# Two banks instead of one for keys, queries and rotary queries, and one step more in a statistic

## The chip, the cores and the metric

The kernel runs on one core of a Trainium2 chip. The time is device microseconds of one execution; before the change the median of three runs is 2838.42 us, from 2837.55 to 2839.09. A core has a matrix engine (TensorE, PE in the rows; PEld is its weight load), VectorE (DVE), ScalarE (ACT), GpSimd (POOL) and SyncE (SP), whose queue issues nearly all transfers. Each engine works its instructions in the order written for it and waits where an operand is not there yet.

## The reference, cut to what matters

Two layers over 256 tokens of width 2048 in float32: a mixer, a convolutional feed-forward network and a gated embedding in each. The change touches the latent attention in the mixer of the first layer:

```python
q = (rmsnorm(cq, q_a_norm) @ w_uq).reshape(b, s, 8, 192)      # 128 plain, 64 rotary
kv = (rmsnorm(ckv, kv_a_norm) @ w_ukv).reshape(b, s, 8, 256)
k_nope, v = kv[..., :128], kv[..., 128:]
k = concat([k_nope, broadcast(kpe)]);  q = rmsnorm(q, q_norm);  k = rmsnorm(k, k_norm)
q, k = rope on the last 64 columns;    o_b = causal_attention(q, k, v)
```

`cq` and `ckv` have 512 columns, so each of these projections sums over four chunks of 128.

## The kernel before, in words

Features lie on the 128 partitions, tokens along the free dimension. A product of float32 quality is made of three products of a shorter format: high weights by high input, high weights by low input, low weights by high input. An input tile holds its high part in columns 0 to 255 and its low part in columns 256 to 511. Weights arrive as blocks of 128 x 1024 (`raw`); ScalarE casts the high part `wh` (line 160, three buffers), VectorE subtracts for the low part `wl` (line 166, four buffers).

Two helpers turn a block into 256 output features. `gemm_fm` (line 174) takes two PSUM banks, one per 128 features: eight products of 512 columns with `wh` (line 190; high and low input at once, so a bank ends with two halves), then eight of 256 columns with `wl` (line 192), at the latest after two blocks. Its result is gathered by `evac` (line 299): per bank ScalarE copies one half to `evt` (line 302) and VectorE adds the other half (line 303). `gemm_fm1` (line 203) takes one bank and issues three products of 256 columns per chunk and half (lines 215, 217, 218), all summed in place; the result can be used as it is. The pool `mm` has five banks.

Work that follows a product is a Python generator. `spawn` starts it, and `pump` lets every live generator take one step; `gemm_fm` pumps after the high products of each block, `gemm_fm1` at the end of each block. `steps(n)` in a generator passes n pumps. `token_stats` (line 358) is such a generator: column sums of squares (`sm_col`, line 368), the power on GpSimd (line 330), diagonal matrices `dg` (line 346), two steps, then two products that spread the row over all partitions (`sm_bc`, line 354). A scheduler then fixes the order of each engine from these pieces; it may place an instruction somewhat before or behind where the text issues it.

The latent attention (`mla`, line 771) goes: values of heads 0 to 3; two rotary-query products (`q_rope`, line 810), each followed by a rotation (`sm_rot`, line 779, then GpSimd and VectorE, lines 309 and 782); then four rounds `up(n)`: keys, queries, and two attention heads spawned. Between the rounds `fill` puts one output product of the other mixer (`xa` by `w_eo0`, 16 high and 16 low products over two blocks). `keys` squares its result on ScalarE (line 836), GpSimd adds the squared rotary key (line 840), TensorE sums the columns (`sm_hs`, line 790); `queries` does the same with two half additions on GpSimd (line 860).

Of the kernel before, what the change touches and what calls it, by code (L numbers as in the profile page):

```python
# [78 lines left out]
def hybrid_kernel(ctx, tc, io):  # L79
# [42 lines left out]
    def spawn(g):  # L122
        if next(g, active) is not active:
            active.append(g)

    def finish():
        while active:
            pump()

    def steps(n):  # L130
        for _ in range(n):
            yield
# [172 lines left out]
    def bcast(row, n=2):  # L305
        return row.unsqueeze(1).to_broadcast([P, n, T])

    def mul(dst, a, b, engine=None):
        (engine or nc.vector).tensor_tensor(dst, a, b, op=ALU.mult)
# [11 lines left out]
    def small(shape, name):  # L321
        return psum.tile(shape, F32, tag="sm", name=name, bufs=3)
# [32 lines left out]
                             start=(half == 0), stop=(half == 1))  # L355
        nc.scalar.copy(dst, ps[:, 0:n * P])

    def token_stats(acc, n, wait=0):

        r = {}  # L360

        def chain():
            yield from steps(wait)
            if acc.shape[1] == 2:
                nc.vector.tensor_tensor(acc[:, 0], acc[:, 0], acc[:, 1], op=ALU.add)
            ps = small([P, 512], "sm_col")
            for m in range(2):
                nc.tensor.matmul(ps[:, m:m + 1], acc[:, 0, m * P:(m + 1) * P], mcol("ones")[:, 0:1],
                                 start=True, stop=True)
            c = rstd_from(ps[:, 0:2], [P, 2], n)  # L370
            r["col"] = c
            dg = diagonals(c, (0, 1))
            yield from steps(2)
            bc = npool.tile([P, T], F32, tag="rbc", name="rbc", bufs=3)
            bcast_rows(dg, bc)
            r["bc"] = bc
        spawn(chain())
        return r
# [293 lines left out]
    def even_mixer(rs, xs):  # L672
# [3 lines left out]
        with tc.tile_pool(name="low", bufs=2) as low:  # L676
            shift(low, "low")
            kpe = low.tile([P, 1, T], F32, name="kpe", bufs=1)
            with tc.tile_pool(name="l0a", bufs=2) as pool:
                hvs = {}  # L680
                done = {}

                def proj(ps, tag, key):
                    yield from until(rs, "bc")
                    y = pool.tile([P, 2, T], F32, tag=tag, name=tag, bufs=2)
                    mul(y, ps, bcast(rs["bc"]))
                    done[key] = y

                def proj_halves(ps, tag, key):
                    yield from until(rs, "bc")  # L690
                    y = pool.tile([P, 2, T], F32, tag=tag, name=tag, bufs=2)
                    evac(ps, y)
                    mul(y, y, bcast(rs["bc"]))
                    done[key] = y

                def values(ps, g):
                    yield from until(rs, "col")
                    hv = pool.tile([P, 2, 512], F32, tag="hv", name="hv", bufs=2)
                    for m in range(2):
                        nc.scalar.activation(hv[:, m], ps[m], AF.Copy, scale=rs["col"][:, m:m + 1])  # L700
                    hvs[g] = hv

                def pair(hp):
                    yield from until(done, (hp, 2))
                    yield from hgrn_pair(pool, hp, done[hp, 0], done[hp, 1], done[hp, 2], lbc, hvs, mix_a)

                lbc = None
                for hp in range(HG_HEADS // 2):
                    if hp == 0:
                        for g, ps in enumerate(first):  # L710
                            spawn(values(ps, g))
                        nc.sync.dma_start(out=mat, in_=io["mat"])
                        nc.vector.tensor_copy(ones_r, mcol("ones"))
                        nc.sync.dma_start(out=vec, in_=io["vec"])
                        lbc = lower_bounds(pool)
                    for k, tag in enumerate(("hf", "hq", "hg")):
                        if hp == 0 and k == 0:
                            spawn(proj(gemm_fm1(io["w_hg"][0], xs), tag, (hp, k)))
                        else:
                            spawn(proj_halves(gemm_fm(io["w_hg"][3 * hp + k], xs), tag, (hp, k)))  # L720
                    if hp == 0:
                        spawn(rope_tables(pool))
                    spawn(pair(hp))


                def low_rank(ps, n, gain, acc, chunks):
                    y = low.tile([P, 2, T], F32, tag="ly", name="ly")
                    evac(ps, y)
                    mul(y, y, bcast(rs["bc"]))
                    if n == 0:  # L730
                        nc.scalar.activation(acc, y, AF.Square)
                    else:
                        sq = npool.tile([P, 2, T], F32, tag="sq", name="sq")
                        nc.scalar.activation(sq, y, AF.Square)
                        nc.vector.tensor_tensor(acc, acc, sq, op=ALU.add)
                    for j in range(2):
                        x = low.tile([P, 2 * T], F32R, name=f"x_{gain}{2 * n + j}", bufs=1)
                        split(x, y[:, j], vcol(gain, 2 * n + j))
                        chunks.append(x)

                stat = {}
                chunks = {"kva": [], "qa": []}
                for part, gain in ((1, "kva"), (0, "qa")):
                    acc = low.tile([P, 2, T], F32, tag="lacc", name="lacc", bufs=1)
                    for n in range(2):
                        low_rank(gemm_fm(io["w_low"][2 * part + n], xs), n, gain, acc, chunks[gain])
                    stat[gain] = token_stats(acc, 512, 2)
                    if part == 1:
                        ps = gemm_fm1(io["w_kpe"], xs, ncol=1, kb=8)
                        mul(kpe, ps, bcast(rs["bc"], 1))  # L750
                while len(mix_a) < HG_HEADS:
                    pump()
                heads_a = iter(range(NC // 2))

                def fill(count=1):

                    for _ in range(count):
                        n = next(heads_a)
                        residual(n, gemm_fm(io["w_eo0"][n], [mix_a[c] for c in range(HG_HEADS)]))

                fill(2)
                finish()
# [9 lines left out]
    def mla(pool, kpe, ckv, cq, rkv, rqa, mix, fill):  # L772
# [37 lines left out]
        def q_rope(ps, g):  # L810
            yield from until(rqa, "bc")
            y = pool.tile([P, 2, T], F32, tag="ly", name="ly")
            mul(y, ps, bcast(rqa["bc"]))
            sq = pool.tile([P, 2, T], F32, name=f"sqr{g}", bufs=1)
            nc.scalar.activation(sq, y, AF.Square)
            nc.scalar.activation(y, y, AF.Copy, scale=vcol("qr"))
            yield
            z = pool.tile([P, 2, T], F32, name=f"qr{g}", bufs=1)
            rotate(z, y)
            for j in range(2):  # L820
                sqr[2 * g + j] = sq[:, j]
                qr[2 * g + j] = z[:, j]
# [8 lines left out]
        def keys(ps, n):  # L831
            yield from until(rkv, "bc")
            y = pool.tile([P, 2, T], F32, tag="ly", name="ly")
            mul(y, ps, bcast(rkv["bc"]))
            sq = npool.tile([P, 2, T], F32, tag="sq", name="sq")
            nc.scalar.activation(sq, y, AF.Square)
            z = pool.tile([P, 2, T], F32, tag="kn", name="kn", bufs=3)
            nc.scalar.activation(z, y, AF.Copy, scale=vcol("kn"))
            lo = sq[0:64]
            nc.gpsimd.tensor_tensor(lo, lo, sqk[0:64].unsqueeze(1).to_broadcast([64, 2, T]), op=ALU.add)  # L840
            yield from steps(2)
            r = pair_rstd(sq, 1.0)
            dg = diagonals(r, (0, 2, 1, 3))
            yield from steps(2)
            rk = pool.tile([P, 2, T], F32, tag="rk", name="rk", bufs=2)
            bcast_rows(dg, rk.rearrange("p a t -> p (a t)"))
            pairs["k", n] = (z, rk)

        def queries(ps, n):
            yield from until(rqa, "bc")  # L850
            y = pool.tile([P, 2, T], F32, tag="ly", name="ly")
            mul(y, ps, bcast(rqa["bc"]))
            sq = npool.tile([P, 2, T], F32, tag="sq", name="sq")
            nc.scalar.activation(sq, y, AF.Square)
            z = pool.tile([P, 2, T], F32, tag="qn", name="qn", bufs=3)
# [57 lines left out]
            mix[hh] = x  # L913

        def up(n):
            spawn(keys(gemm_fm1(io["w_uk"][n], ckv), n))
            spawn(queries(gemm_fm1(io["w_uq"][n], cq), n))
            for j in range(2):
                spawn(attention(n, j, 2 * j))

        spawn(values(gemm_tm(io["w_uv"][0], ckv), 0))
        for g in range(2):
            spawn(q_rope(gemm_fm1(io["w_uqr"][g], cq), g))
        up(0)
        fill()
        up(1)
# [286 lines left out]
```

## Time and profile before

| what | value |
|---|---|
| median of three runs | 2838.42 us |
| the profiled execution's own time | 2838.33 us |
| its span, first to last instruction | 2836.5 us |
| TensorE busy | 2828.3 us (100%) |
| VectorE busy | 1904.7 us (67%) |
| ScalarE busy | 1412.2 us (50%) |
| GpSimd busy | 85.8 us (3%) |
| mean granted TensorE clock | 1.000 |

The profile comes from one execution. A busy time counts an engine as occupied from an instruction's start to its end; matmuls overlap each other, so the pace of TensorE is read from start to start and not from the length of one. In a wait, the name behind the arrow is the work that ended last before the waiting one could start.

### The profile page before, as it was taken

The page shows a single profiled execution, that of the slowest core. Times are in us where ns is not written, and L with a number is a line of the kernel's source. Part 1 is how long each engine was busy: PE and PEld are TensorE (multiplying, and loading weights), DVE is VectorE, ACT ScalarE, POOL GpSimd, SP SyncE. Part 2 cuts the span into 40 slices and gives each one's busy share as a digit, 9 for nine tenths or more (in the row PEclk, how much of TensorE's full clock was granted, in tenths as well). Part 3 has the DMA queues.
Part 4 walks back from the last instruction along what each step waited for, and adds up shares of the span by engine and source line. Part 5 has one row for each costly group of instructions (what it writes and reads, how often), then busy time and mean ns, then how long its engine had stood idle before and what let it go on. Part 6 is the DMA issues. An engine that isn't in the chain of part 4 may idle for free.

```text
span 2836.5 us, 41173 instructions
## 1 busy us (share of the span) xinstructions
PE 2828.3 (100%) x15993; PEld 2471.9 (87%) x15993; DVE 1904.7 (67%) x2777; ACT 1412.2 (50%) x1864; POOL 85.8 (3%) x123
## 2 busy tenths in 40 slices
PE   9999999999999999999999999999999999999999
PEld 7888888888888888888888888888888888888888
DVE  7876787766557666776565555556777755777666
ACT  5765555444344444565544444455444433444444
POOL 1110300000000000000000000000000000000000
PEclk9999999999999999999999999999999999999999
DMA  7545445665656665565555555555656665566565
GB/s 240 179 156 164 133 154 187 192 192 189 190 188 192 192 189 190 182 196 182 184 182 187 189 187 186 185 183 183 193 186 193 192 190 190 186 193 193 186 193 164
DMA packets 147941, 525.60 MB, mean 185 GB/s; under 512 B 16544, under 2 KB 18336, under 8 KB 147744
## 3 DMA queue, kind: packets, MB, share of 16 engines
q1 hardware_dynamic: 147600, 522.95, 58.2%
q8 instruction: 125, 2.05, 0.3%
q14 instruction: 72, 0.59, 0.1%
q10 hardware_dynamic: 144, 0.01, 0.0%
HBM read 520.80 MB, written 2.10 MB: 184 GB/s over the span
## 4 chain that ended last, share of the span: by engine, by line
PE 98%; DVE 1%; DMA 0%; issue 0%; ACT 0%; POOL 0%; SPq 0%; DVEq 0%
PE mm L190 52%; PE mm L192 27%; PE mm L235 4%; PE mm L234 4%; PE mm L236 4%; PE sm_ro L1015 1%; PE mm L215 0%; PE mm L218 0%; PE mm L217 0%; PE mm L271 0%; PE mm L272 0%; PE mm L270 0%; DVE wl L166 0%; PE sm_sc L881 0%; PE sm_rt L1029 0%; PE sm_sc L880 0%
## 5 line engine op out<-in xcount | busy, mean ns | idle before, releaser
L160 ACT CAST wh<-raw 128x1024 fp32r<-128x1024 f32 (+1 forms) x990 | 1032.5, 1044 | 1196.2 <-PE mm L190 766.3
L166 DVE TENSOR_TENSOR wl<-raw,wh 128x1024 fp32r<-128x1024 f32 (+1 forms) x848 | 1025.2, 1217 | 646.4 <-ACT wh L160 629.6
L190 PE MATMUL mm<-xs,wh 128*128 128x512 f32 x4288 | 1028.9, 391 | 0.1
L190 PEld LDWEIGHTS mm<-xs,wh 128*128 128x128 f32 x4288 | 787.2, 188 | 153.2 <-DVE xs L318 0.4
L192 PEld LDWEIGHTS mm<-xs,wl 128*128 128x128 f32 x4288 | 541.4, 189 | 19.1
L192 PE MATMUL mm<-xs,wl 128*128 128x256 f32 x4288 | 550.9, 281 | 0.0
L190 PE MATMUL mm<-hs,wh 128*128 128x512 f32 x1408 | 337.2, 391 | 0.0
L190 PEld LDWEIGHTS mm<-hs,wh 128*128 128x128 f32 x1408 | 258.2, 188 | 49.6
L166 DVE TENSOR_TENSOR wlt<-raw,wh 128x1024 fp32r<-128x1024 f32 x142 | 175.4, 1236 | 145.6 <-PE mm L235 124.3
L234 PE MATMUL mm<-wh,xs 128*128 128x512 f32 x512 | 199.7, 390 | 0.0
L235 PE MATMUL mm<-wlt,xs 128*128 128x512 f32 x512 | 199.3, 389 | 0.0
L236 PE MATMUL mm<-wh,xs 128*128 128x512 f32 x512 | 199.2, 389 | 0.0
L192 PEld LDWEIGHTS mm<-hs,wl 128*128 128x128 f32 x1408 | 179.4, 189 | 7.3
L192 PE MATMUL mm<-hs,wl 128*128 128x256 f32 x1408 | 181.7, 281 | 0.0
L302 ACT COPY evt<-mm 128x256 f32<-128x256 f32 x300 | 98.3, 375 | 92.1 <-PE mm L192 92.1
L190 PE MATMUL mm<-xo,wh 128*128 128x512 f32 x512 | 122.7, 391 | 0.0
L236 PEld LDWEIGHTS mm<-wh,xs 128*128 128x128 f32 x512 | 96.1, 188 | 20.0
L234 PEld LDWEIGHTS mm<-wh,xs 128*128 128x128 f32 x512 | 96.1, 188 | 19.5
L235 PEld LDWEIGHTS mm<-wlt,xs 128*128 128x128 f32 x512 | 96.2, 188 | 19.4
L190 PEld LDWEIGHTS mm<-xo,wh 128*128 128x128 f32 x512 | 94.0, 188 | 18.5 <-DVE xo L1032 0.3
L406 DVE TENSOR_TENSOR h<-h,mm 128x256 f32<-128x256 f32 x128 | 48.2, 416 | 37.2 <-PE mm L192 37.2
L192 PEld LDWEIGHTS mm<-xo,wl 128*128 128x128 f32 x512 | 64.9, 189 | 2.5
(283 smaller groups left out, 2040.4 us busy)
## 6 DMA issues: line engine op xcount, KB each, us to landing
raw<-in_wg SPq DMA_DIRECT2D x176, 512.0 KB, 3.7
raw<-in_wu SPq DMA_DIRECT2D x176, 512.0 KB, 4.0
raw<-in_wd SPq DMA_DIRECT2D x176, 512.0 KB, 3.8
raw<-in_w_oqk SPq DMA_DIRECT2D x64, 512.0 KB, 4.0
raw<-in_w_ov SPq DMA_DIRECT2D x64, 512.0 KB, 3.6
raw<-in_w_og SPq DMA_DIRECT2D x64, 512.0 KB, 3.6
raw<-in_w_oo SPq DMA_DIRECT2D x64, 512.0 KB, 3.9
raw<-in_wpg SPq DMA_DIRECT2D x60, 512.0 KB, 3.8
```

The costliest lines, as they stand in the source:

```text
L160: nc.scalar.copy(wh, raw)
L166: nc.vector.tensor_tensor(wl, raw, wh.bitcast(F32), op=ALU.subtract)
L190: nc.tensor.matmul(ps[j], w[:, o:o + P], xs[kc], start=(kc == 0), stop=False)
L192: nc.tensor.matmul(ps[j][:, 0:T], w[:, o:o + P], xs[kc][:, 0:T], start=False, stop=(kc == n - 1))
L234: nc.tensor.matmul(ps[m], xh, wh[:, o:o + 512], start=(kc == 0), stop=False)
L235: nc.tensor.matmul(ps[m], xh, wl[:, o:o + 512], start=False, stop=False)
L236: nc.tensor.matmul(ps[m], xl, wh[:, o:o + 512], start=False, stop=(kc == n - 1))
L302: nc.scalar.copy(tmp[:, j], ps[j][:, T:2 * T])
L406: nc.vector.tensor_tensor(h[i][:, j], h[i][:, j], ps[j][:, 0:T], op=ALU.add)
L1015: nc.tensor.matmul(pso, at[:, c, o:o + P], v[:, b, s], start=(n == 0), stop=(n == len(terms) - 1))
```

## The change

Three edits. `token_stats` takes the number of its inner steps as an argument, and the statistic of the keys and values (`kva`, part 1) passes three instead of two. The products of keys, queries and rotary queries (four, four and two of them, one block each) go from `gemm_fm1` to `gemm_fm`: two banks, eight products of 512 columns and eight of 256 where there were 24 of 256. Their three consumers get the two halves, so each gathers them with `evac` first and multiplies the gathered tile in SBUF, where it multiplied the bank directly.

```diff
-    def token_stats(acc, n, wait=0):
+    def token_stats(acc, n, wait=0, more=2):
...
-            yield from steps(2)
+            yield from steps(more)
...
-                    stat[gain] = token_stats(acc, 512, 2)
+                    stat[gain] = token_stats(acc, 512, 2, 3 if part == 1 else 2)
...
         def q_rope(ps, g):
             yield from until(rqa, "bc")
             y = pool.tile([P, 2, T], F32, tag="ly", name="ly")
-            mul(y, ps, bcast(rqa["bc"]))
+            evac(ps, y)
+            mul(y, y, bcast(rqa["bc"]))
...
         def keys(ps, n):
-            mul(y, ps, bcast(rkv["bc"]))
+            evac(ps, y)
+            mul(y, y, bcast(rkv["bc"]))
...
         def queries(ps, n):
-            mul(y, ps, bcast(rqa["bc"]))
+            evac(ps, y)
+            mul(y, y, bcast(rqa["bc"]))
...
         def up(n):
-            spawn(keys(gemm_fm1(io["w_uk"][n], ckv), n))
-            spawn(queries(gemm_fm1(io["w_uq"][n], cq), n))
+            spawn(keys(gemm_fm(io["w_uk"][n], ckv), n))
+            spawn(queries(gemm_fm(io["w_uq"][n], cq), n))
...
-            spawn(q_rope(gemm_fm1(io["w_uqr"][g], cq), g))
+            spawn(q_rope(gemm_fm(io["w_uqr"][g], cq), g))
```

Outside the stretch from this statistic to the end of the attention heads, each engine's order is as before. Three places of it follow; line numbers behind line 810 are one to three higher in the changed kernel.

TensorE at the statistic of keys and values, before: `sm_bc` spreads the row, `xs` by `wh` and `wl` are high and low products of the next low-rank projection.

```order
L368 MATMUL sm_col<-mat,lacc 128x1 x2
L190 MATMUL mm<-xs,wh 128x512 x16
L192 MATMUL mm<-xs,wl 128x256
L354 MATMUL sm_bc<-dg,ones_r 128x256
L192 MATMUL mm<-xs,wl 128x256 x2
L354 MATMUL sm_bc<-dg,ones_r 128x256
L192 MATMUL mm<-xs,wl 128x256 x13
```

The same place in the changed kernel:

```order
L368 MATMUL sm_col<-mat,lacc 128x1 x2
L190 MATMUL mm<-xs,wh 128x512 x16
L192 MATMUL mm<-xs,wl 128x256 x16
L190 MATMUL mm<-xs,wh 128x512 x8
L354 MATMUL sm_bc<-dg,ones_r 128x256 x2
```

The two spreading products stand 15 low and eight high products later.

TensorE from the end of the first queries into the first `fill`, before: `xa` is the fill, the first `sm_hs` the column sums of the first keys, the second those of the first queries.

```order
L218 MATMUL mm<-x_qa_2740,wl 128x256
L190 MATMUL mm<-xa,wh 128x512 x8
L790 MATMUL sm_hs<-mat,sq 128x1 x4
L190 MATMUL mm<-xa,wh 128x512 x8
L790 MATMUL sm_hs<-mat,sq 128x1 x4
L192 MATMUL mm<-xa,wl 128x256 x16
```

In the changed kernel, from the second rotation on (`sm_rot`, which stood ahead of the queries' products before):

```order
L779 MATMUL sm_rot<-ly,mat 128x512
L190 MATMUL mm<-x_qa_2634,wh 128x512
L190 MATMUL mm<-x_qa_2737,wh 128x512 x2
L190 MATMUL mm<-x_qa_2740,wh 128x512 x2
L192 MATMUL mm<-x_qa_2631,wl 128x256 x2
L192 MATMUL mm<-x_qa_2634,wl 128x256 x2
L192 MATMUL mm<-x_qa_2737,wl 128x256 x2
L192 MATMUL mm<-x_qa_2740,wl 128x256 x2
L190 MATMUL mm<-xa,wh 128x512 x9
L790 MATMUL sm_hs<-mat,sq 128x1 x4
L190 MATMUL mm<-xa,wh 128x512 x7
L192 MATMUL mm<-xa,wl 128x256 x6
```

The second rotation has moved behind the third product of the queries (the first one, likewise, behind the ninth product of the keys), while the keys' sums stand nine products into the fill, where it was eight.

VectorE in the same stretch, before: `ly<-mm,rbc` is the multiplication of a finished projection, `qr` the rotation, `wl` a weight block.

```order
L309 TENSOR_TENSOR ly<-mm,rbc 128x512
L309 TENSOR_TENSOR qr_2987<-sm_rot,sin_mla 128x512
L166 TENSOR_TENSOR wl<-raw,wh 128x1024
L782 TENSOR_TENSOR qr_2987<-qr_2987,ly 128x512
L309 TENSOR_TENSOR ly<-mm,rbc 128x512
L309 TENSOR_TENSOR qr_3029<-sm_rot,sin_mla 128x512
L166 TENSOR_TENSOR wl<-raw,wh 128x1024
L782 TENSOR_TENSOR qr_3029<-qr_3029,ly 128x512
```

In the changed kernel, where `ly<-mm,evt` is the addition of `evac` and `ly<-ly,rbc` the multiplication:

```order
L309 TENSOR_TENSOR qr_2970<-sm_rot,sin_mla 128x512
L166 TENSOR_TENSOR wl<-raw,wh 128x1024
L782 TENSOR_TENSOR qr_2970<-qr_2970,ly 128x512
L309 TENSOR_TENSOR qr_3010<-sm_rot,sin_mla 128x512
L303 TENSOR_TENSOR ly<-mm,evt 128x256
L782 TENSOR_TENSOR qr_3010<-qr_3010,ly 128x512
L303 TENSOR_TENSOR ly<-mm,evt 128x256
L309 TENSOR_TENSOR ly<-ly,rbc 128x512
```

The first keys' multiplication, the last row here, stood ahead of the second rotation's two VectorE instructions and now stands behind them.

## Rows read from the trace of the kernel before

**Rows 1.** The page: busy time by engine; the chain that ended last, by engine.
```profile
PE 2828.3 (100%) x15993; PEld 2471.9 (87%) x15993; DVE 1904.7 (67%) x2777; ACT 1412.2 (50%) x1864; POOL 85.8 (3%) x123
...
PE 98%; DVE 1%; DMA 0%; issue 0%; ACT 0%; POOL 0%; SPq 0%; DVEq 0%
```

**Rows 2.** Waits of TensorE, whole span: total us, times, longest.
```profile
PE spin L99 <- DVE cold L96: 1.1, 1, 1.1
...
PE sm_bc L354 <- DVE dg L346: 0.6, 1, 0.6
```

**Rows 3.** Timeline of TensorE at the statistic: start, length, instruction, idle before.
```profile
243.32 0.28 PE L192 MATMUL mm<-xs,wl 128*128 128x256 f32 x1
244.23 0.35 PE L354 MATMUL sm_bc<-dg,ones_r 128*128 128x256 f32 x1 [0.63 <-DVE dg L346]
```

**Rows 4.** Timeline of VectorE at the same place.
```profile
244.00 0.48 DVE L346 TENSOR_SCALAR dg<-mat,rl 128x128 fp32r<-128x128 f32 x2
```

**Rows 5.** Timeline of TensorE in an undisturbed stretch of the two-bank product.
```profile
389.82 3.82 PE L190 MATMUL mm<-xb,wh 128*128 128x512 f32 x16
393.48 2.05 PE L192 MATMUL mm<-xb,wl 128*128 128x256 f32 x16
395.36 3.82 PE L190 MATMUL mm<-xb,wh 128*128 128x512 f32 x16
```

**Rows 6.** Timeline of TensorE: rotary queries, first rotation, first keys, the keys' sums.
```profile
281.13 0.28 PE L218 MATMUL mm<-x_qa,wl 128*128 128x256 f32 x1
...
286.55 1.02 PE L779 MATMUL sm_rot<-ly,mat 128*128 128x512 f32 x2
...
287.52 0.28 PE L217 MATMUL mm<-x_kva,wh 128*128 128x256 f32 x1
...
295.76 0.95 PE L790 MATMUL sm_hs<-mat,sq 128*128 128x1 f32 x8
```

**Rows 7.** Windows: stretch, its length, busy us of PE, PEld, DVE, ACT, POOL, clock, DMA.
```profile
280.00:290.00 10.00, 10.00 (x78) 9.38 (x76) 7.19 (x10) 6.88 (x9) 2.04 (x2) 1.00 0.50 159
```

**Rows 8.** Timeline of VectorE, from the last low-rank projection to the first fill.
```profile
263.46 0.75 DVE L303 TENSOR_TENSOR ly<-mm,evt 128x256 f32<-128x256 f32 x2
264.24 0.69 DVE L309 TENSOR_TENSOR ly<-ly,rbc 128x512 f32<-128x512 f32 x1
...
287.61 0.69 DVE L309 TENSOR_TENSOR qr<-sm_rot,sin_mla 128x512 f32<-128x512 f32 x1 [0.17 <-PE sm_rot L779]
288.21 1.82 DVE L166 TENSOR_TENSOR wl<-raw,wh 128x1024 fp32r<-128x1024 f32 x1
289.96 0.68 DVE L782 TENSOR_TENSOR qr<-qr,ly 128x512 f32<-128x512 f32 x1
...
293.64 1.77 DVE L782 TENSOR_TENSOR qr<-qr,ly 128x512 f32<-128x512 f32 x1
```

**Rows 9.** Timeline of ScalarE, same stretch.
```profile
251.93 0.65 ACT L302 COPY evt<-mm 128x256 f32<-128x256 f32 x2 [0.72 <-PE mm L192]
...
283.80 1.05 ACT L160 CAST wh<-raw 128x1024 fp32r<-128x1024 f32 x1 [1.51 <-PE mm L217]
...
285.42 0.73 ACT L816 ACTIVATE ly<-ly,vec 128x512 f32<-128x512 f32 x1
...
291.47 0.63 ACT L836 ACTIVATE sq<-ly 128x512 f32<-128x512 f32 x1
```

**Rows 10.** Timeline of GpSimd, from the second rotation into the second round.
```profile
291.34 1.30 POOL L309 TENSOR_TENSOR ly<-ly,cos_mla 128x512 f32<-128x512 f32 x1 [2.38 <-PE sm_rot L779]
292.60 2.26 POOL L840 TENSOR_TENSOR sq<-sq,sqk 64x512 f32<-64x512 f32 x1
296.75 1.79 POOL L860 TENSOR_TENSOR sq<-sq,sqr 64x256 f32<-64x256 f32 x2 [1.90 <-ACT sq L854]
298.62 1.01 POOL L330 TENSOR_TENSOR rr<-rv,mat 128x4 f32<-128x4 f32 x1
...
307.77 1.48 POOL L840 TENSOR_TENSOR sq<-sq,sqk 64x512 f32<-64x512 f32 x1 [4.10 <-ACT sq L836]
```

## The prediction

> **What bounds the kernel now.** I read the page first. TensorE is busy all the time, and the chain that ended last is its own to 98% [rows 1]. So nothing counts but what TensorE issues, at what pace, and where it stands still; VectorE, ScalarE and GpSimd cost only where they make it wait. The waits of TensorE came next: over the whole span the largest is 1.1 us in total, at the very start, and one of 0.6 us stands before the spreading product of a statistic [rows 2]. There is therefore little to win by removing waits, and any new wait is paid in full. Then the timeline: TensorE at the statistic [rows 3] and in the two kinds of product [rows 5, 6], and the other three engines where the changed projections are consumed [rows 7 to 10]. There the reader is to see that VectorE (7.19 of 10 us) and ScalarE (6.88) have some three microseconds of room in ten [rows 7].
>
> All sums are made against the profiled execution, 2838.33 us; the median of the three runs is 0.09 us more, which I neglect.
>
> **The step more in the statistic.** From the low product at 243.32 to the spreading product at 244.23 pass 0.91 us [rows 3]. The pace of such products is 0.12 us: sixteen take 395.36 - 393.48 = 1.88 us [rows 5]. So 0.79 us are lost, to the diagonals, which end at 244.48 [rows 4]. In the changed order the pair stands 15 low and eight high products later, 15 x 0.1175 + 8 x 0.229 = 3.6 us after 243.4, at about 247.0, when the diagonals have long been there. The row that it makes is first used on the keys' product, which begins at about 287 [rows 6], 40 us later, so nothing is late next. Gain 0.79 us, whole.
>
> **Ten products in two banks.** One block was 24 products of 256 columns. From 281.13 to 286.55 there are 46 starts in 5.42 us, 0.1178 us each [rows 6], 2.83 us a block. Now there are eight of 512 columns, (393.48 - 389.82) / 16 = 0.229 us each, and eight of 256 at 0.1175 [rows 5]: 2.77 us. That is 0.057 us a block, 0.57 us for ten. The columns are as many as before; only starts are saved.
> The Trainium skill, page "TensorE: Matmul & The Clock Gate", section "Back-to-back issue gap", gives an isolated warm gap of N/2.4 + 2.5 ns, 109 and 216 ns here; by an estimate from it a block would save 0.02 us and the ten 0.2 us. The starts measured here are dearer (118 and 229 ns), so I keep 0.57.
>
> **What the gathering adds.** Per projection, two copies on ScalarE (0.65 us [rows 9]) and two additions on VectorE (0.75 [rows 8]); the multiplication stays at 0.69. In the densest stretch, two rotary products, first keys and first queries in some 11 us, this is 3.0 us for VectorE, whose room is about as large. Weights are prepared more than a block ahead (the cast at 283.80 [rows 9] is of the queries' block, which follows the keys of 287.52 [rows 6]), and low products now come behind eight high ones, 1.83 us, so I cost weights at nothing; what hides them is that lead. What I do not cost at nothing are the chains from one projection's result to the next TensorE instruction that needs it, since the order has the latter at nearly the same place:
>
> First rotation. It needs ScalarE's scaled tile. ScalarE, in its order: a weight cast that can begin when the second rotary product's last high product is done (0.39 after its start: 3.82 - 15 x 0.229 [rows 5]), cast 1.05, copy 0.33, square 0.63, copy 0.33, scale 0.73 [rows 9]: 3.46 us. TensorE in that time: 0.23 + 0.94 (eight low) + 1.83 (eight high of the keys) + 0.12 (one low) = 3.12. It waits 0.34 us (0.1 to 0.6).
>
> Keys' sums, round one. The keys' multiplication now stands on VectorE behind the second rotation's addition, and that waits for GpSimd. From the start of the second rotation: result to dependent 287.61 - 286.55 = 1.06 [rows 6, 8], GpSimd 1.30 [rows 10], addition 0.68, gathering addition 0.38, multiplication 0.69 [rows 8], square 0.63 [rows 9], GpSimd's addition 1.48 to 2.26 [rows 10]: 6.2 to 7.0 us. TensorE: the rotation 0.85 (287.52 - 286.55 less one start [rows 6]), five high 1.15, eight low 0.94, nine high of the fill 2.06: 5.0 us. It waits 1.2 to 2.0 us, up to 2.5 if the weight block ahead of it on VectorE is slowed as at 288.21 (1.82) [rows 8]. I take 1.7, since a weight block starts on VectorE just before GpSimd's addition, as where that took 2.26. Behind the waiting sums stand the rest of the fill and everything after: nothing overtakes.
>
> Queries' sums, round one. GpSimd now computes the keys' power before the queries' additions, and the power waits for the keys' sums. From their end: 1.01 + 1.79 [rows 10] and about 0.5 of hand-overs (estimate: half of the 1.06 us above), 3.3 us; TensorE has seven high, six and two low products and a sum, 1.60 + 0.94 + 0.2 = 2.7. It waits 0.5 (0 to 0.8).
>
> Round two. The queries' gathering stands on VectorE behind an instruction that waits for the keys' sums: 0.5 + 0.75 + 0.69 + 0.63 + 1.79 = 4.4 us to the queries' sums, against five high products, three transposes (0.4, estimate by the 0.95 of the sums' eight [rows 6]) and fifteen low, 3.3. It waits 1.0 (0 to 2.0). Rounds three and four have a whole product or more between these points, by the order 5 to 8 us against chains of 4 to 6 (estimates with the same durations): nothing (0 to 1.5 each).
>
> Banks: five, two a projection now. The fill's second bank is the keys' first, freed 2.1 to 2.9 us after the second rotation; TensorE is there after 2.94. Nothing, but without spare.
>
> Sum: -0.79 - 0.57 + 0.34 + 1.7 + 0.5 + 1.0 = +2.2 us, 2838.33 + 2.2 = 2840.5 us. With the lower ends of the waits (0.1 + 1.2) it is 2838.3, with the upper ones (0.6 + 2.5 + 0.8 + 2.0 + 3.0 = 8.9) 2845.9.
>
> **The rivals.**
> Covers hold: the sums find their operands ready and only the gains stay, 2838.33 - 1.36 = 2837.0 us. For it: before the change GpSimd's addition ended at 294.86 and the sums started at 295.76 [rows 6, 10], 0.9 us of room. Against it: the chain is longer by two rows on VectorE and a wait for GpSimd. Chance 0.15.
>
> Rounds three and four wait as well, 1.0 us each: 2842.5 us. For it: VectorE is given 0.75 us more in each projection; against it: the transposes, scores and outputs that stand between. Chance 0.12.
>
> Slower: VectorE and GpSimd stop each other. A rotation addition took 0.68 us at 289.96 and 1.77 at 293.64, where GpSimd's addition ran beside it, and a weight block took 1.82 beside GpSimd's 1.30 [rows 8, 10]. The ten multiplications took a bank and an SBUF tile and now take two SBUF tiles. If each meets GpSimd and stands on the path, 10 x 1.09 = 10.9 us more, 2851 us; it decides from four of the ten on (2.2 + 4.4 us is beyond 0.2%). Against it: GpSimd works 85.8 us in all [rows 1], and the next chain often waits for the multiplication, so that GpSimd is idle then. Chance 0.07.
> The Trainium skill, "SBUF — State Buffer", section "Who interferes with whom", says that a VectorE instruction with two SBUF inputs contends with a GpSimd instruction that reads SBUF, and one with a bank as input does not; the 1.77 and 1.82 us agree with it, and by it the change trades ten free instructions for ten exposed ones.
>
> The forecast itself, some waits on the sums of rounds one and two: chance 0.66, its own range 2838.3 to 2842.5.
>
> **How the numbers follow.** The three runs spread 1.5 us; 0.2%, 5.7 us, is about what a measurement can tell from no change. Forecast and the first two rivals lie within it. Slower by more is the third, 0.07; faster by more has no mechanism here, with 1.4 us of gains and no wait above 1.1 us left to remove [rows 2], and gets 0.02 for what I overlook; 0.91 is left. The range goes from the first rival, 2836.9, to 2843.4, short of the upper ends' sum.
>
> **What the profile of the changed kernel would show.** The spreading pair without idle time before it; blocks of keys and queries 2.77 us long; a gap of some 0.3 us before the first rotation; keys' sums of round one starting 1 to 2 us after the ninth product of the fill, released by GpSimd; less before the queries' sums of rounds one and two. If those sums start at once, the first rival is right; if gaps follow in rounds three and four, or multiplications of 1.5 us and more appear, the others. A gap before a `wh` or `wl` product would show that the weights' lead did not last.

## The result, and the profile of the changed kernel

The changed kernel takes 2843.32 us in the median of 16 runs (2842.20 to 2845.42); the kernel before, run beside it on the same chip, 2838.19 us (16 runs, 2837.34 to 2839.65). The ratio is 1.0019, with a 95% interval of 1.0012 to 1.0026. The change makes the kernel 5.1 us slower; 2.2 us were forecast. The profiled execution took 2844.31 us with a span of 2842.5 us, 6.0 us more than the span before. The difference of the medians is a little smaller, and the changed kernel's runs scatter more; a reason for the scatter comes with the experiments. Three single runs in the experiments below, of 4160 us and more, are left out of every ratio.

The page first: busy time by engine, and the chain that ended last, by engine.

```profile
PE 2831.7 (100%) x15913; PEld 2471.3 (87%) x15913; DVE 1913.6 (67%) x2797; ACT 1417.9 (50%) x1884; POOL 86.4 (3%) x123
...
PE 97%; DVE 1%; issue 1%; POOL 1%; DMA 0%; ACT 0%; SPq 0%; POOLq 0%; DVEq 0%
```

Against [rows 1] TensorE has 80 products fewer and yet is busy 3.4 us longer, and GpSimd has come into the chain. Fewer products that take longer is the first sign of something that the forecast had no term for. The waits of TensorE over the whole span (total us, times, longest):

```profile
PE sm_hs L790 <- POOL sq L842: 2.5, 1, 2.5
PE sm_hs L790 <- POOL sq L863: 1.1, 3, 0.5
```

The wait of 0.6 us before the spreading product [rows 2] is gone, and 3.6 us of waits on GpSimd before the head sums (`sm_hs`) are new. The timeline of TensorE shows them in place; the columns are start, length, instruction, and idle time before it:

```profile
247.21 0.40 PE L354 MATMUL sm_bc<-dg,ones_r 128*128 128x256 f32 x2
...
287.63 0.28 PE L192 MATMUL mm<-x_kva,wl 128*128 128x256 f32 x1
287.84 1.13 PE L779 MATMUL sm_rot<-ly,mat 128*128 128x512 f32 x2
...
290.32 1.03 PE L779 MATMUL sm_rot<-ly,mat 128*128 128x512 f32 x2
...
293.26 2.23 PE L190 MATMUL mm<-xa,wh 128*128 128x512 f32 x9
297.94 1.62 PE L790 MATMUL sm_hs<-mat,sq 128*128 128x1 f32 x8 [2.45 <-POOL sq L842]
299.42 3.33 PE L190 MATMUL mm<-xa,wh 128*128 128x512 f32 x7
302.56 1.48 PE L192 MATMUL mm<-xa,wl 128*128 128x256 f32 x6
303.83 0.42 PE L790 MATMUL sm_hs<-mat,sq 128*128 128x1 f32 x2
...
305.46 1.17 PE L192 MATMUL mm<-xa,wl 128*128 128x256 f32 x8
306.47 0.86 PE L190 MATMUL mm<-x_kva,wh 128*128 128x512 f32 x3
...
311.77 2.00 PE L190 MATMUL mm<-x_qa,wh 128*128 128x512 f32 x8
...
314.56 2.00 PE L190 MATMUL mm<-xa,wh 128*128 128x512 f32 x8
...
324.19 0.38 PE L790 MATMUL sm_hs<-mat,sq 128*128 128x1 f32 x2 [0.47 <-POOL sq L863]
...
325.06 0.83 PE L790 MATMUL sm_hs<-mat,sq 128*128 128x1 f32 x6 [0.27 <-POOL sq L863]
325.75 0.48 PE L234 MATMUL mm<-wh,x_kva 128*128 128x512 f32 x1
...
368.28 0.83 PE L790 MATMUL sm_hs<-mat,sq 128*128 128x1 f32 x6 [0.38 <-POOL sq L863]
```

The reader is to see two things. The keys' sums of round one begin at 297.94, where nine products from 293.26 at 0.229 us each [rows 5] would have brought them to 295.32: 2.6 us of standing still. (The profile's 2.45 counts from the modelled end of the last product.) And behind that wait the same instructions are slow: seven products of 512 columns occupy 299.42 to 302.56, 0.449 us each, where the eight at 311.77 are done in the usual 2.00 us. The windows show why (stretch, length, busy us of PE, PEld, DVE, ACT, POOL, granted clock, DMA):

```profile
290.00:300.00 10.00, 7.55 (x37) 5.86 (x36) 8.55 (x13) 5.72 (x11) 4.43 (x4) 0.91 0.35 119
300.00:310.00 10.00, 10.00 (x47) 8.55 (x45) 7.07 (x19) 2.49 (x3) 4.25 (x4) 0.75 0.19 54
```

The same stretches in the kernel before:

```profile
290.00:300.00 10.00, 10.00 (x68) 8.87 (x67) 7.41 (x12) 6.58 (x8) 6.25 (x5) 1.00 0.50 158
300.00:310.00 10.00, 10.00 (x74) 8.92 (x73) 7.76 (x22) 2.78 (x4) 4.08 (x3) 1.00 0.41 126
```

The granted clock, 1.00 in both stretches before, is 0.91 and then 0.75 of full speed here. A full clock is 2.4 GHz and the lower level 1.2, so 0.09 and 0.25 missing of ten microseconds are 1.8 and 5.0 us at the lower level: 6.8 us, from about 298.2, right behind the wait, to about 305.0. The low products at 305.46 are at their usual pace again (eight in 1.17 us, with one change of product before them). The page's row of 40 slices doesn't show it, since each slice is 71 us long.

What made the sums late stands on the other engines. VectorE, then GpSimd, then ScalarE, same columns:

```profile
289.61 1.82 DVE L166 TENSOR_TENSOR wl<-raw,wh 128x1024 fp32r<-128x1024 f32 x1
...
293.22 0.69 DVE L782 TENSOR_TENSOR qr<-qr,ly 128x512 f32<-128x512 f32 x1 [0.26 <-POOL ly L309]
293.83 0.42 DVE L303 TENSOR_TENSOR ly<-mm,evt 128x256 f32<-128x256 f32 x1
294.28 0.69 DVE L309 TENSOR_TENSOR ly<-ly,rbc 128x512 f32<-128x512 f32 x1
...
296.69 1.75 DVE L309 TENSOR_TENSOR ly<-ly,rbc 128x512 f32<-128x512 f32 x1
```

```profile
291.44 1.75 POOL L309 TENSOR_TENSOR ly<-ly,cos_mla 128x512 f32<-128x512 f32 x1 [1.09 <-PE sm_rot L779]
295.71 2.17 POOL L842 TENSOR_TENSOR sq<-sq,sqk 64x512 f32<-64x512 f32 x1 [2.53 <-ACT sq L838]
```

```profile
295.00 0.63 ACT L838 ACTIVATE sq<-ly 128x512 f32<-128x512 f32 x1 [0.86 <-DVE ly L309]
```

From the second rotation (290.32) to the sums (297.94) the chain takes 7.62 us. It is link by link the one that the forecast laid out, with the rotation's GpSimd part at 1.75 us where [rows 10] had 1.30.

A ledger by four places in TensorE's order, each start compared with its start before: the first fill product of round one comes 0.66 us earlier than before (293.26 against 293.92), the first keys' product of round two 5.21 us later (306.47 against 301.26), and the first products behind round two's sums 6.51 us later (325.75 against 319.24); at the end it is 6.0. The three starts before:

```profile
293.92 2.00 PE L190 MATMUL mm<-xa,wh 128*128 128x512 f32 x8
...
301.26 0.28 PE L215 MATMUL mm<-x_kva,wh 128*128 128x256 f32 x1
...
319.24 0.40 PE L234 MATMUL mm<-wh,x_kva 128*128 128x512 f32 x1
```

So the loss is made in two places: 5.87 us in round one's sums, 1.30 us in round two's; everything behind gives back 0.5 us net.

### The profile page after: what moved, and what is told of

The parts are those of the page before. It is cut to its first block, busy times and chain, and to the rows that moved or that the text cites. A ratio compares the mean times of both kernels' runs of the same rounds, so it can differ in the third digit from the quotient of the medians.

```text
span 2842.5 us, 41055 instructions
## 1 busy us (share of the span) xinstructions
PE 2831.7 (100%) x15913; PEld 2471.3 (87%) x15913; DVE 1913.6 (67%) x2797; ACT 1417.9 (50%) x1884; POOL 86.4 (3%) x123
## 4 chain that ended last, share of the span: by engine, by line
PE 97%; DVE 1%; issue 1%; POOL 1%; DMA 0%; ACT 0%; SPq 0%; POOLq 0%; DVEq 0%
PE mm L190 53%; PE mm L192 27%; PE mm L234 4%; PE mm L235 4%; PE mm L236 4%; PE sm_ro L1018 1%; PE mm L271 0%; PE mm L272 0%; PE mm L270 0%; PE sm_rt L1032 0%; PE sm_ra L994 0%; PE sm_sc L884 0%; DVE wl L166 0%; DMA raw<-in_w_hv 0%; PE sm_o L648 0%
## 5 line engine op out<-in xcount | busy, mean ns | idle before, releaser
L302 ACT COPY evt<-mm 128x256 f32<-128x256 f32 x320 | 104.7, 374 | 96.6 <-PE mm L192 96.6
```

The source lines that it names most:

```text
L302: nc.scalar.copy(tmp[:, j], ps[j][:, T:2 * T])
```

## The experiments

All kernels are timed in five rounds beside the kernel before, whose median was 2838.34 us with the first four (the step alone, the idle products, the longer GpSimd work, the sums one step later), 2838.04 with the next four (the banks alone, the longer work with idle products, the addition on VectorE, four steps and three) and 2838.21 with the other two (rotary queries in one bank, four steps and two). Theory: a wait of 2.6 us and a clock that falls behind it. Rivals: the two-bank products are slow in themselves, or the work of the other engines is.

**The step alone.** The kernel before with only the step more in the statistic.

```
-    def token_stats(acc, n, wait=0):
+    def token_stats(acc, n, wait=0, more=2):
...
-            yield from steps(2)
+            yield from steps(more)
...
-                    stat[gain] = token_stats(acc, 512, 2)
+                    stat[gain] = token_stats(acc, 512, 2, 3 if part == 1 else 2)
```

> The kernel before with the step more in the key-value statistic and nothing else. Both theories (the loss is the wait for the first keys' sums plus the slow clock behind it; or the loss belongs to the two-bank products and their gathering as such) give the gain of the prediction's first term, 0.8 us: 2837.4 us against 2838.2, no idle time before the spreading pair, clock 1.00 throughout. If the step only moved the wait elsewhere: 2838.2.

Measured: 2837.23 us (11 runs, 2836.63 to 2838.99), ratio 0.9997 [0.9988, 1.0005], span 2835.2 us, no wait before the spreading product. The medians are 1.1 us apart where 0.79 was worked out; the interval can't tell this from nothing, but the sign agrees and the wait is gone.

**The banks alone.** The changed kernel with the statistic as before.

```
-                    stat[gain] = token_stats(acc, 512, 2, 3 if part == 1 else 2)
+                    stat[gain] = token_stats(acc, 512, 2)
```

> The two-bank products without the step more in the statistic. If the parts add, the time is the changed kernel's 2843.3 plus the 0.8 to 1.1 us that the step alone took off (0.79 in the rows of before, 1.1 in the run of the step alone): 2844.2 us, with the wait ahead of the keys' sums of round one near 2.6 us, the clock at its lower level for some microseconds behind it, and the statistic's wait back. Rival: the step itself has a part in the loss (the keys' sums' work is late because the statistic ended elsewhere); then this kernel stands at or below 2842.0 us.

Measured: 2844.76 us (2842.83 to 2845.93), ratio 1.0023 [1.0013, 1.0032]. The wait of 2.4 us is there, but the clock doesn't fall right behind it:

```profile
299.77 1.05 PE L790 MATMUL sm_hs<-mat,sq 128*128 128x1 f32 x8 [2.45 <-POOL sq L842]
300.68 1.87 PE L190 MATMUL mm<-xa,wh 128*128 128x512 f32 x7
...
303.79 0.38 PE L790 MATMUL sm_hs<-mat,sq 128*128 128x1 f32 x2 [0.56 <-POOL sq L863]
...
306.58 3.31 PE L190 MATMUL mm<-x_kva,wh 128*128 128x512 f32 x8
```

The seven products at 300.68 keep the usual pace, and the clock is 1.00 in every microsecond up to 305. It falls at about 306.0, six microseconds behind that wait and two behind one of 0.56 us before the queries' sums, and stays down for 3.4 us. The two parts of the change add up within the scatter of the runs, and the whole loss belongs to the banks.

**Idle products in the wait.** The changed kernel, with 22 small bf16 products into a spare bank ahead of the keys' sums of round one.

```
+            if n == 0:
+                idle = small([P, T], "sm_id")
+                for _ in range(22):
+                    nc.tensor.matmul(idle, cold[:, 0:P], cold, start=True, stop=True)
```

> The changed kernel with 22 products of zeros (bf16, 256 columns, into a PSUM tile that nothing reads) ahead of the keys' sums of round one, so that TensorE works through most of the 2.5 us in which it stood still. The chain to the sums is as long as before. Theory wait-and-clock: the sums start at the same time, but the clock stays at its high level, and about 2.8 us come back: 2840.5 us, clock 1.00 in the ten microseconds behind the sums. Rival (the clock falls, or the time goes, because of the two-bank products, the gathering or VectorE and GpSimd stopping each other): 2843.3 us and the clock near 0.75 there, as in the changed kernel.

Measured: 2841.67 us (2840.67 to 2844.31), ratio 1.0013 [1.0004, 1.0022]. The clock is 1.00 from 290 to 310. But it falls one round later:

```profile
314.08 0.70 PE L888 MATMUL sm_sc<-kr,qr 64*128 64x256 f32 x2
315.10 1.05 PE L790 MATMUL sm_hs<-mat,sq 128*128 128x1 f32 x8 [0.32 <-POOL sq L842]
316.01 3.45 PE L190 MATMUL mm<-xa,wh 128*128 128x512 f32 x8
```

Eight products take 3.45 us instead of 2.00, behind small score products and a wait of 0.32 us; the window from 310 to 320 has a clock of 0.83. Half a confirmation: the slow products left the place where the standstill was filled, and the time came down by 1.7 us of the 2.8 expected; in the profiled run the clock fell elsewhere.

**The other way round: the wait without the banks.** The kernel before, one-bank products, with two GpSimd operations more on the keys' squares of round one, which cancel each other. Then the same with 26 small products that TensorE carries out meanwhile.

```
+            if n == 0:
+                late = pool.tile([P, 2, T], F32, name="late", bufs=1)
+                nc.gpsimd.tensor_tensor(late[0:64], lo, sqk[0:64]..., op=ALU.subtract)
+                nc.gpsimd.tensor_tensor(lo, late[0:64], sqk[0:64]..., op=ALU.add)
```

The second kernel has these and, behind them:

```
+            if n == 0:
+                idle = small([P, T], "sm_id")
+                for _ in range(26):
+                    nc.tensor.matmul(idle, cold[:, 0:P], cold, start=True, stop=True)
```

> The kernel before, one-bank products and the old statistic, with two more GpSimd operations (subtract and add back the same operand) on the keys' squares of round one, 2.6 to 4.4 us, of which 0.9 us are covered. TensorE's order is as before. Theory wait-and-clock: TensorE waits 1.7 to 3.5 us at the keys' sums and the clock then falls as in the changed kernel: 2838.2 + 2.6 + 2.8 = 2843.6 us. Rival (the fall of the clock belongs to the two-bank products): only the wait is paid, 2839.9 to 2841.7 us, clock 1.00 throughout.

> The kernel before with two GpSimd operations more on the keys' squares of round one, as in the earlier run of 2844.3 us, and 26 small bf16 products into a spare bank that TensorE carries out while it would stand still ahead of the keys' sums. The sums are as late as in that run, 3.1 us; what differs is that TensorE isn't idle meanwhile. If the clock falls from the standstill, it holds here and the time is 2838.3 + 3.1 = 2841.4 us. If the loss beyond the wait comes from GpSimd's longer work elsewhere, the time is 2844.3 us again.

Measured: 2844.33 us without the small products (2841.82 to 2846.10), ratio 1.0020 [1.0011, 1.0029]; 2840.74 us with them (2840.10 to 2841.06), ratio 1.0009 [1.0000, 1.0018]. TensorE's timeline of the first, then of the second:

```profile
298.55 1.05 PE L790 MATMUL sm_hs<-mat,sq 128*128 128x1 f32 x8 [2.91 <-POOL sq L844]
299.46 3.29 PE L190 MATMUL mm<-xa,wh 128*128 128x512 f32 x8
...
305.70 0.28 PE L215 MATMUL mm<-x_kva,wh 128*128 128x256 f32 x1
```

```profile
294.99 3.01 PE L849 MATMUL sm_id<-cold 128*128 128x256 bf16 x26
298.05 1.05 PE L790 MATMUL sm_hs<-mat,sq 128*128 128x1 f32 x8
298.97 2.08 PE L190 MATMUL mm<-xa,wh 128*128 128x512 f32 x8
...
303.62 0.28 PE L215 MATMUL mm<-x_kva,wh 128*128 128x256 f32 x1
```

And a window of each, the first kernel's and the second's:

```profile
300.00:310.00 10.00, 10.00 (x62) 9.09 (x61) 6.78 (x20) 2.44 (x3) 2.94 (x2) 0.83 0.31 97
```

```profile
300.00:310.00 10.00, 10.00 (x72) 8.85 (x71) 6.93 (x21) 3.82 (x5) 3.71 (x4) 1.00 0.33 106
```

This is the cleanest pair. The sums are equally late in both, 8.60 us behind the second rotation (289.95 in the first, 289.45 in the second), and GpSimd does the same work; only TensorE is idle in the one and busy in the other. The eight products behind take 3.29 us there and 2.08 here, and the clock is 0.83 there and 1.00 here. From the sums to the first keys' product of round two pass 7.15 us there and 5.57 here, so in the traces standing still costs 1.6 us beyond the standstill itself, without any two-bank projection. In the medians it is more: the loss against the kernel before is 6.0 us there and 2.7 us here, 3.3 us apart. The profiled run of the first, 2842.17 us, is among its quickest; the slower ones have no trace, so why they lose more is not shown. Their clock hints at a longer fall: in the first kernel four runs with a mean granted clock of 0.998 took 2844.3 to 2846.1 us, seven with 0.999 took 2841.8 to 2844.6. In the second all eleven have 1.000 and lie within 1.0 us. In the changed kernel, too, the six runs with 0.998 took 2843.3 to 2845.4 us, the ten with 0.999 2842.2 to 2844.3.

**The sums later.** The changed kernel, with one step of other columns more ahead of the keys' and of the queries' sums of round one.

```
-            yield from steps(2)
+            yield from steps(3 if n == 0 else 2)
```

> The changed kernel with one step more ahead of the keys' and the queries' sums of round one; the keys' sums then stand 16 products into the fill where they stood nine. Theory wait-and-clock: TensorE comes 1.6 us later and waits about 1.0 us, the queries' sums wait for nothing, the clock holds: 2843.3 - 1.6 - 2.8 - 0.2 = 2838.7 us; should a wait of 1.0 us be enough to lower the clock, 2841.5. Rival (two-bank products and gathering as such): the wait shrinks but the rest stays, 2841.5 us or more.

Measured: 2837.74 us (2837.29 to 2839.28), ratio 0.9998 [0.9989, 1.0007]. The wait is still there, a third as long, and in the profiled run the clock holds (the two slowest of the eleven runs, 2839.1 and 2839.3 us, have a mean clock of 0.999, the others 1.000):

```profile
292.29 3.81 PE L190 MATMUL mm<-xa,wh 128*128 128x512 f32 x16
297.00 1.05 PE L790 MATMUL sm_hs<-mat,sq 128*128 128x1 f32 x8 [0.89 <-POOL sq L842]
```

**One instruction off GpSimd.** The changed kernel, with the keys' addition of round one on VectorE.

```
-            nc.gpsimd.tensor_tensor(lo, lo, sqk[0:64]..., op=ALU.add)
+            (nc.vector if n == 0 else nc.gpsimd).tensor_tensor(lo, lo, sqk[0:64]..., op=ALU.add)
```

> The changed kernel, with one instruction of the keys' chain in round one on VectorE instead of GpSimd: the addition of the shared squared keys, which takes GpSimd 2.17 us in the changed kernel's trace and should take VectorE 0.4 to 0.8 us. If the wait and the clock that falls behind it are the cause, the wait ahead of the keys' sums shrinks from 2.6 us to about 1.0 us, the clock stays at its upper level there, and the time is 2843.3 minus 1.6 minus 2.8 = 2838.9 us (2838 to 2839.5). If the clock falls for another reason than that wait (the two-bank products themselves), only the wait's 1.6 us go and the time is 2841.7 us. If GpSimd isn't the late one, nothing goes: 2843.3 us.

Measured: 2844.02 us (2841.41 to 2845.31), ratio 1.0019 [1.0010, 1.0029]. The expectation failed, though the wait did shrink:

```profile
295.54 1.05 PE L790 MATMUL sm_hs<-mat,sq 128*128 128x1 f32 x8 [0.70 <-DVE sq L842]
...
299.53 0.38 PE L790 MATMUL sm_hs<-mat,sq 128*128 128x1 f32 x2 [1.21 <-POOL sq L863]
...
301.27 1.44 PE L790 MATMUL sm_hs<-mat,sq 128*128 128x1 f32 x6 [1.01 <-POOL sq L863]
```

What was won before the keys' sums is lost before the queries': their additions (`sq L863`) stand on GpSimd behind the keys' power, took 2.45 us for two, and had been hidden by the keys' own lateness. The clock fell during the second of these two waits, at about 301.1; the window from 300 to 310 has 0.66. I had looked at one wait and not at who came next in GpSimd's queue.

**Rotary queries in one bank again.**

```
-            evac(ps, y)
-            mul(y, y, bcast(rqa["bc"]))
+            mul(y, ps, bcast(rqa["bc"]))
...
-            spawn(q_rope(gemm_fm(io["w_uqr"][g], cq), g))
+            spawn(q_rope(gemm_fm1(io["w_uqr"][g], cq), g))
```

> The changed kernel with the rotary queries in one bank again, as before; keys and queries keep two banks. If the late point is VectorE's queue behind the second rotation, the two gathering additions and the two copies of the rotary queries that are gone there make the keys' sums of round one wait less: about 1.3 us instead of 2.6 (six microseconds of products stand between by the order, against a chain of 7.1 to 7.6). A run with a wait of 1.05 us there kept its clock, so the time is 2843.3 - 1.3 - 2.8 + 0.1 = 2839.3 us (0.1 us for two blocks of products that are long again). Rival: the keys' and queries' own gathering makes the chain late; then the wait stays at 2.4 us or more, the clock falls behind it, and the time is 2843 us or more.

Measured: 2843.02 us (2841.16 to 2846.32), ratio 1.0018 [1.0009, 1.0027]. The same miss. The wait before the keys' sums is 1.35 us, as expected, but 1.0 us appears before the queries' sums, and the clock falls there (0.83 from 300 to 310). So the rotary queries' gathering is about half of the keys' lateness; keys and queries alone still lose the time.

**Four steps in round one, with two or three in round two.**

```
-            yield from steps(2)
+            yield from steps(4 if n == 0 else 2)
```

The second kernel:

```
-            yield from steps(2)
+            yield from steps(4 if n == 0 else 3 if n == 1 else 2)
```

> As the kernel with sums moved four steps in round one, without the move in round two (two steps there, as in the changed kernel). If the two small waits ahead of round two's queries' sums (1.15 us together in the changed kernel) belong to round two alone, they come back and the time is 2836.5 + 1.15 = 2837.7 us. If they are an echo of round one's lateness, they don't, and it is 2836.5 us. In both cases no wait stands before the sums of round one, and the clock holds.

> The changed kernel with the sums taken later: four steps of other columns ahead of the keys' and the queries' sums of round one, three ahead of those of round two, where there were two. By the theory no sum waits for GpSimd any more, the clock stays at its upper level, and what remains of the change is its gain: 0.8 to 1.1 us for the statistic and 0.6 us for the ten blocks, so 2836.6 us (2836.0 to 2837.3). Rival: what is late moves to the scores of round one, which wait for the sums' results; then they wait about 1 us and the time is 2837.7 us or more.

Measured: 2838.82 us for the first (2837.69 to 2840.67), ratio 1.0002 [0.9993, 1.0011]. Round two's waits came back, 0.88 and 0.41 us, and in the profiled execution the clock fell behind them (0.83 from 310 to 320), so it lost 1.1 us more than expected. The second takes 2836.51 us (2835.76 to 2837.52), ratio 0.9994 [0.9986, 1.0003], as expected: the clock is 1.000 in all eleven runs, no wait before any sum is left, and the page has TensorE at 99% of the chain:

```profile
PE 2827.0 (100%) x15913; PEld 2467.2 (87%) x15913; DVE 1911.0 (67%) x2797; ACT 1418.3 (50%) x1884; POOL 88.2 (3%) x123
...
PE 99%; DVE 1%; DMA 0%; ACT 0%; SPq 0%; issue 0%
```

The same 15913 products that kept TensorE busy for 2831.7 us in the changed kernel take 2827.0 us here. This version is the fastest of all in its median, 1.5 us under the kernel before; the interval still reaches past one.

## Why the prediction was wrong

The forecast was a small loss within 0.2%, from waits before the head sums. The loss is small and from those waits, and the time lies inside the range; but it is 5.1 us, not 2.2, and the measurement tells it from no change: the interval is 3.4 to 7.4 us, where the forecast took 5.7 us for about the least that can be told. That the time still lies in the range, 0.1 us under its upper end, is luck: a cost stands in it that the forecast did not have. By its steps:

- The statistic: right. The pair stands at 247.21 (247.0 worked out) with nothing before it; 0.79 us worked out, 1.1 between the medians of the step alone.
- The ten blocks: right as far as seen. A block of queries runs from 311.77 to 314.56, 2.79 us, where 2.77 was worked out.
- First rotation: 0.34 forecast, 0.09 found (the low product at 287.63 is followed by the rotation at 287.84, with 0.12 the usual distance).
- Keys' sums, round one: the mechanism was right, the size was not. 1.7 taken, 2.6 found. TensorE's side was 5.0 us as worked out; the chain took 7.62, where a wait of 1.7 implies 6.7. Half of the 0.9 between them is the rotation's GpSimd part, 1.75 against the 1.30 of [rows 10]; the rest is GpSimd's addition (2.17, where about 1.95 is implied) and the hand-overs. The weight block did take 1.82, for which "up to 2.5" was given, but it was off the path: VectorE had to wait 0.26 us for GpSimd behind it (293.22).
- Queries' sums, round one: 0.5 taken, about 0.2 found, but at the lower clock, at which TensorE came to them later. In the run of the banks alone, where the clock still held there, the wait was 0.56 us.
- Round two: 1.0 taken; two waits of 0.47 and 0.27 us found, 1.2 us together by the starts, and the ledger has 1.30. Rounds three and four: nothing taken, and one wait of 0.38 us found, in round four (368.28).
- The failing step is the sum. It prices a wait at its own length ("any new wait is paid in full") and every product behind it at the pace of [rows 5], which was measured at the full clock. Behind the 2.6 us wait the clock was at its lower level for 6.8 us, and that cost about as much as the wait: of the 5.87 us lost between the fill and round two's keys, 2.6 are the wait, some 0.2 the queries', and the remaining 3.0, by difference, the clock. The pair with and without idle products measures such a fall alone: 1.6 us in the traces, for 3.4 us at the lower level, and 3.3 us between the medians. With the waits as found and 3.0 for the clock the sum is -0.79 - 0.57 + 0.09 + 2.6 + 0.2 + 1.2 + 3.0 = +5.7 us, 2844.1 beside the 2844.31 of the profiled run. The median run lost 1.0 us less; it has no trace.

The Trainium skill, page "TensorE: Matmul & The Clock Gate", section "HAM oscillation — how this bites in real kernels", counts the cost of a throttled stretch as half its length; by an estimate from it 6.8 us cost 3.4, near the 3.0 that the starts give here. The forecast read this page for the pace of products and not for this.

Of the rivals, that the covers hold is refuted by the waits; that rounds three and four wait 1.0 us each by the single 0.38 us found there; and that VectorE and GpSimd stop each other all over by TensorE's ledger: behind round two nothing more is lost net. At single places the two engines are slow side by side: the queries' multiplication of round one took 1.75 us beside GpSimd's addition, which took 2.17. The multiplication is not on the way to the keys' sums, but GpSimd's addition is, and its length is part of the first wait.

What stays open: which wait makes the clock fall, and how soon. It fell behind single waits of 2.5 and 2.9 us, 0.3 and 1.5 us after TensorE had gone on; in the run of the banks alone it held for six microseconds behind the 2.5 us and fell behind a further 0.56 us. It fell behind 0.7, 1.2 and 1.0 us within seven microseconds, behind 1.3 and 1.0 us some five apart, behind 0.9 and 0.4 us shortly after small score products, and behind 0.3 us right after such products in one run. It held behind 0.9 us among wide products in a profiled run. The runs don't give a rule for the small ones, and the moment of the fall differs between kernels with the same first wait. What the pair shows is that the standstill is the cause there, not what sets the moment.

## What to carry to other kernels

On an engine that is never idle, price a new wait at its length and then ask what the engine's clock does behind it; here a wait of 2.6 us cost 5.6 in the profiled run. Read the granted clock in windows of ten microseconds, since the page's 40 slices hide it, and treat a count of products that falls while busy time rises as its sign. When a wait on a shared engine is shortened, look at what stands next in that engine's queue; moving the consumer later in TensorE's own order removed the waits of both, while speeding up one producer only passed the wait on.

## What the runs showed of the hardware

- The lower clock followed standstills of 2.5 to 2.9 us, in the run of the banks alone only six microseconds later and behind a second wait. It stayed for 6.8 us in the profiled runs of the changed kernel and of the addition on VectorE, and for 3.4 us in those of the longer GpSimd work, the banks alone, the idle products, the rotary queries in one bank, and four steps and two. Products of 512 columns then start 0.427 us apart instead of 0.229 (317.93, 318.36, 318.79 and 319.21 in the run with four steps and two).
- Small bf16 products with no use, in the place of the standstill, kept the clock at its upper level there, and the pair of kernels that differ in them alone is 3.3 us apart in the medians, 1.6 us in the stretch behind the sums in the traces.
- Kernels whose mean granted clock is 1.000 in every run repeat within 1.0 to 2.5 us; those in which most or many runs have less spread over 3 to 5 us. A wider spread of times was itself a sign of the cause.
